# One product on VectorE takes the merge gates out of PSUM, in place of a ScalarE copy and a GpSimd product

## The chip, the cores and the metric

The kernel runs on one core of a Trainium2 chip. The metric is the device time of one execution in microseconds (us). The kernel before was run three times: 1630.13, 1631.73 and 1632.48 us, median 1631.73. The profile below is of one execution more.

TensorE is called PE here, VectorE DVE, ScalarE ACT, GpSimd POOL and SyncE SP, as the profile does. SP issues the DMA transfers.

## The reference

One decoder layer on x of 1024 tokens by 1024 channels, in float32: native sparse attention (NSA, three branches: compressed, selected, window) beside gated linear attention (GLA), both merged by per-channel gates, then a SwiGLU channel mixer. Cut to what matters for the change:

```
h = rmsnorm(x, gain)                       # rbc below: 1 / rms of each token
... = split(h @ w_in)                      # q, k, v, gates of both mixers, and g_merge (2 * 1024 columns)
o_a = nsa_attention(q, ...)                # 8 heads, 2 groups, query blocks of 128
o_b = gla(...)                             # chunk by chunk
gate_a, gate_b = split(sigmoid(g_merge))
merged = gate_a * (o_a @ w_up_nsa) + gate_b * (o_b @ w_up_gla)
x = x + merged @ w_out
```

The change concerns g_merge alone: its product with the weights stands in PSUM without the factor 1/rms of each token. It is multiplied by that factor and parked in DRAM until the merge takes the sigmoid of it.

## The kernel before, in words

Everything is laid out with channels on the 128 partitions and tokens along the row; a token row of 1024 is worked on in two halves of 512 (`hf`). Weights and activations are split in a high and a low part (`wh`, `wl`, `hh`, `hl`) so that float32 products are made of three matmuls. `dense` and `products` (L370 to L415) make a list of such work: a half of a job is 8 blocks of 3 matmuls of 128x512 (line L405) into one PSUM bank, then a call of `evac`, which takes the bank's content away and returns the word "pause". Each quarter of a job also loads weights (DMA), splits them by an ACT copy (L354) and a POOL subtraction (L355).

`gate_job(j)` is one job of this kind. For j below 4 it makes another gate, of the GLA mixer; for j of 4 to 19 it makes 128 channels of g_merge. Its `evac` copies PSUM to an SBUF tile `zt` on ACT (L926), multiplies it in place by `rbc`, 128x512, on POOL (L927), and stores it to DRAM on SP's queue (L928). There are 16 such jobs, 32 halves: two halves run in the GLA stage, two in the query stage (about 366 to 376 us), and 28 in the attention stage after it, up to about 738 us.

In the attention stage the merge gates are fill: PE works on them where attention isn't ready. The order of PE's work there is written by `Plan` (L107 to L236). It walks through 16 units of attention (2 groups of 8 query blocks) and keeps a simple model of when ACT, DVE and POOL will be done (`on`, `free`), with fixed costs in ns. At each step it takes a transpose (`turn`), scores (`score`) or a value product (`value`) that its model says is ready; where none is ready within 300 ns, it takes the next fill matmul. Fill has one PSUM bank, `d`; after the last matmul of a half ("pause") the plan gives no more fill until its model says that the bank is free (`self.d`). PE's order is fixed as `Plan` wrote it; the order on the other engines is made by a scheduler when the program is built, and each engine works through its own queue in order.

What attention puts on the engines, by lines of the profile: scores on PE into a bank of `s` (L1060 and L1061; L1040 for the compressed branch); maximum `nm` on DVE (L1101, L1088); exponential on ACT (L1103); reciprocal and weight `rr` on DVE (L1071, L1076); scaled `p` on DVE (L1079) or ACT (L1077); transposes on PE into one of two banks `t` (L1139, L1123); their split into `pth` by an ACT copy (L1116) and `ptl` by a DVE subtraction that reads the same bank (L1117); value products on PE (L1148, L1131). A bank `t` comes free when `ptl` is done. For each unit four casts on DVE (L1009) and POOL operations prepare the rotated queries `qs`.

Behind the attention stage the rest of the fill is worked off, then the merge reads the gates back from DRAM.

Of the kernel before, what the change touches and what calls it, by code (L numbers as in the profile page):

```python
# [14 lines left out]
AF = mybir.ActivationFunctionType  # L15
OP = mybir.AluOpType
AX = mybir.AxisListType.X

T, D, DFF = 1024, 1024, 2816
# [52 lines left out]
class Fill:  # L72
# [8 lines left out]
    def run(self, ns):  # L81
        self.credit += ns
        while self.q and self.credit > 0:
            cost, fn = self.q.popleft()
            self.credit -= cost
            fn()
        if not self.q:
            self.credit = 0.0
# [12 lines left out]
LAT, WAIT, LOADED = 155.0, 300.0, 1500.0  # L101
# [5 lines left out]
class Plan:  # L107
# [109 lines left out]
    def run(self):  # L217
        ops = dict(T=(self.turn_at, self.turn), S=(self.score_at, self.score), P=(self.value_at, self.value))
        while self.scores or self.turns or self.pend:
            at = {k: ops[k][0]() for k in ops}  # L220
            now = [k for k in ops if at[k] is not None and at[k] <= self.t]
            if now:
                ops[now[0]][1]()
                continue
            nxt = min((v, k) for k, v in at.items() if v is not None)
            if self.fill.q and self.d <= self.t and nxt[0] > self.t + WAIT:
                cost, fn = self.fill.q.popleft()
                self.t += cost
                said = fn()
                if said == "pause":  # L230
                    self.d = self.on("A", self.t, 478.0) + LAT
                elif said in ("part", "load"):
                    self.d = self.t + (LOADED if said == "load" else LOADED / 2)
                    self.on("A", self.t + 2500.0, 1040.0)
                continue
            self.t = nxt[0] if not self.fill.q or nxt[0] <= self.t + WAIT else min(nxt[0], self.d)  # L236
# [3 lines left out]
def layer_kernel(ctx, tc, a, outT):  # L240
    nc = tc.nc
    V, S, P, PE, SP = nc.vector, nc.scalar, nc.gpsimd, nc.tensor, nc.sync
# [54 lines left out]
    def mid(nm, dt=F32, shape=(512,)):  # L297
        return cur["pool"].tile([128, *shape], dt, name=nm, tag=cur["tag"], bufs=cur["bufs"])
# [10 lines left out]
    def hs(hf):  # L309
        return slice(512 * hf, 512 * (hf + 1))  # L310
# [148 lines left out]
    def log_sigmoid(out, z):  # L459
        S.activation(out, z, AF.Abs)  # L460
        S.activation(out, out, AF.Exp, scale=-1.0)
        S.activation(out, out, AF.Ln, bias=1.0)
        V.scalar_tensor_tensor(out, z, 0.0, out, op0=OP.min, op1=OP.subtract)
# [15 lines left out]
    rbc = cst.tile([128, 1024], F32, name="rbc")  # L479
# [83 lines left out]
    def proj(evac, bank=ps_m, fine=False):  # L563

        def make(getw):
            out = []
            for hf in range(2):
                out += products(getw, bank, hhf[hf], hlf[hf], 0,
                                lambda p, hf=hf: evac(p, hf), fine)
            return out  # L570
        return make
# [344 lines left out]
    def gate_job(j, bank=ps_m, fine=False):  # L916
        def evac(p, hf):
            t = mid("zt")
            if j < 4:
                e = mid("ze")  # L920
                V.tensor_mul(t, p, rbc[:, hs(hf)])
                log_sigmoid(e, t)
                S.activation(e, e, AF.Exp)
                P.tensor_tensor(t, t, e, OP.mult)
            else:
                S.activation(t, p, AF.Copy)  # L926
                P.tensor_tensor(t, t, rbc[:, hs(hf)], OP.mult)  # L927
            SP.dma_start(zd[j, :, hs(hf)], t)  # L928
        return a["w_t"][12 + j], proj(evac, bank, fine)

# [27 lines left out]
    for n, (h, hf) in enumerate(pieces):  # L958
# [14 lines left out]
        t = tz[:, 0, :]  # L973
# [772 lines left out]
```

## Time and profile before

| what | value |
|---|---|
| median of the runs | 1631.73 us (1630.13 to 1632.48) |
| the profiled execution: its own time | 1633.16 us |
| its span in the trace | 1631.4 us, so 1.76 us lie outside it |
| PE busy in the span | 1579.5 us, 97% |
| DVE, ACT, POOL busy in the span | 64%, 50%, 46% |
| attention stage (370 to 745 us): PE, DVE, ACT, POOL | 362.8, 274.2, 250.0, 154.2 us of 375 |

How to read it: an engine that is busy 97% leaves 3% in which it waited, and only there can a change of what the other engines do be seen in the time, as long as PE's own work stays the same. The view of waits says for each instruction how long its engine sat idle before it and whose end released it.

### The profile page before, as it was taken

Reading aid. Unit: us, or ns where it says so; the run is one execution under the profiler, and the core shown is the slowest. Engines: PE = TensorE matmul, PEld = TensorE weight load, DVE = VectorE, ACT = ScalarE, POOL = GpSimd, SP = SyncE. Lnnn points to the kernel's source line nnn. Section 1 sums busy time; section 2 is a strip of 40 time slices with the busy share of each in tenths; the row PEclk is TensorE's granted clock in tenths of the full one; section 3 lists DMA queues with packets and bytes.
Section 4 is the critical chain, followed back from the end, with each engine's and each line's share of the span. In section 5 each row is a group of like instructions: output and inputs, shape, how many; then the busy total and the mean of one; then the engine's idle time right before and its main releaser. Section 6 shows DMA issues by size and latency. Waiting matters only on the chain.

```text
span 1631.4 us, 23119 instructions
## 1 busy us (share of the span) xinstructions
PE 1579.5 (97%) x8047; PEld 1315.6 (81%) x8047; DVE 1050.3 (64%) x1704; ACT 815.4 (50%) x1643; POOL 747.0 (46%) x668
## 2 busy tenths in 40 slices
PE   9999999999999999998999999999999999999997
PEld 6888988887888878886777878888888888888886
DVE  7781587594876787778455477744444444499776
ACT  6132567454776666667644444333333334444542
POOL 6110376563333443434135440465666666646560
PEclk9999999999999999999999999999999999999999
DMA  5331122441111111121266541322332332695414
GB/s 196 112 100 57 61 67 70 132 149 62 44 45 46 53 49 40 36 89 64 92 200 231 188 155 56 128 101 98 103 100 101 103 104 97 218 369 162 142 43 145
DMA packets 107782, 179.85 MB, mean 110 GB/s; under 512 B 12033, under 2 KB 26770, under 8 KB 107666
## 3 DMA queue, kind: packets, MB, share of 16 engines
q1 hardware_dynamic: 104354, 172.35, 31.8%
q10 hardware_dynamic: 3312, 6.03, 1.0%
q8 instruction: 63, 1.03, 0.3%
q14 instruction: 53, 0.43, 0.1%
HBM read 130.36 MB, written 47.97 MB: 109 GB/s over the span
## 4 chain that ended last, share of the span: by engine, by line
PE 65%; DVE 7%; DMA 4%; ACT 4%; issue 3%; POOL 1%; SPq 1%; DVEq 0%; POOLq 0%; ACTq 0%
PE m L405 10%; PE m L1358 9%; PE m L1359 9%; PE m L1360 9%; PE d L405 7%; PE t L1139 3%; PE m L1675 3%; PE m L1677 3%; PE o L1148 3%; PE m L1676 3%; PE s L1060 2%; DVE qs L1009 1%; PE s L1061 1%; DMA ar<-actd 1%; DVE ptl L1117 1%
## 5 line engine op out<-in xcount | busy, mean ns | idle before, releaser
L355 POOL TENSOR_TENSOR wl<-wf,wh 128x512 fp32r<-128x512 f32 x106 | 146.1, 1382 | 295.4 <-ACT wh L354 267.8
L1358 PE MATMUL m<-xt,wh 128*128 128x512 f32 x412 | 161.4, 392 | 2.6 <-ACT sc L1364 2.6
L1360 PE MATMUL m<-xt,wl 128*128 128x512 f32 x412 | 160.3, 389 | 0.0
L1359 PE MATMUL m<-xt,wh 128*128 128x512 f32 x412 | 160.3, 389 | 0.0
L1291 POOL TENSOR_TENSOR wl<-ws,wh 128x512 fp32r<-128x512 f32 x76 | 107.4, 1418 | 91.2 <-ACT wh L1290 69.5
L1117 DVE TENSOR_TENSOR ptl<-t,pth 128x512 fp32r<-128x512 f32 (+1 forms) x168 | 99.6, 597 | 48.0 <-ACT pth L1116 44.8
L1291 POOL TENSOR_TENSOR wl<-wr,wh 128x512 fp32r<-128x512 f32 x69 | 91.6, 1328 | 58.5 <-ACT wh L1290 57.5
L1291 POOL TENSOR_TENSOR wl<-wd,wh 128x512 fp32r<-128x512 f32 x56 | 83.0, 1486 | 62.3 <-ACT wh L1290 62.1
L1290 ACT ACTIVATE wh<-wr 128x512 fp32r<-128x512 f32 x87 | 54.8, 630 | 111.8 <-POOL wl L1291 79.1
L1675 PE MATMUL m<-xb,wh 128*128 128x512 f32 x280 | 109.5, 391 | 0.3 <-DVE g L1405 0.3
L1291 DVE TENSOR_TENSOR xb<-ar,xb 128x512 fp32r<-128x512 f32 (+1 forms) x84 | 85.1, 1029 | 38.1 <-ACT xb L1290 37.9
L1677 PE MATMUL m<-xb,wl 128*128 128x512 f32 x280 | 109.3, 390 | 0.2 <-POOL wl L1291 0.2
L1676 PE MATMUL m<-xb,wh 128*128 128x512 f32 x280 | 109.0, 389 | 0.0
L354 ACT ACTIVATE wh<-wf 128x512 fp32r<-128x512 f32 x106 | 66.2, 627 | 82.0 <-PE m L405 48.3
L1116 ACT ACTIVATE pth<-t 128x512 fp32r<-128x512 f32 (+1 forms) x168 | 88.0, 526 | 37.1 <-PE t L1139 35.1
L1290 ACT ACTIVATE wh<-ws 128x512 fp32r<-128x512 f32 x76 | 47.9, 630 | 112.2 <-PE m L1359 93.1
L405 PE MATMUL m<-hh,wh 128*128 128x512 f32 x240 | 102.0, 425 | 0.0
L1139 PE MATMUL t<-ident,p 128*128 128x128 f32 x528 | 83.9, 276 | 13.1 <-DVE ptl L1117 13.0
L1358 PEld LDWEIGHTS m<-xt,wh 128*128 128x128 f32 x412 | 77.3, 188 | 22.1 <-ACT sc L1364 6.4
L405 PE MATMUL m<-hh,wl 128*128 128x512 f32 x240 | 94.1, 392 | 0.0
L405 PE MATMUL m<-hl,wh 128*128 128x512 f32 x240 | 93.9, 391 | 0.0
L1360 PEld LDWEIGHTS m<-xt,wl 128*128 128x128 f32 x412 | 77.3, 188 | 16.3
(385 smaller groups left out, 4657.1 us busy)
## 6 DMA issues: line engine op xcount, KB each, us to landing
ar<-actd SPq DMA_DIRECT2D x70, 256.0 KB, 3.1
wf<-in_w_t SPq DMA_DIRECT2D x58, 256.0 KB, 2.9
wr<-in_w_gate SPq DMA_DIRECT2D x44, 256.0 KB, 2.7
wr<-in_w_upf SPq DMA_DIRECT2D x44, 256.0 KB, 2.7
zd<-zt SPq DMA_DIRECT2D x40, 256.0 KB, 2.0
wd<-in_w_down SPq DMA_DIRECT2D x33, 256.0 KB, 5.2
wf<-in_w_out SPq DMA_DIRECT2D x32, 256.0 KB, 3.1
actd<-t SPq DMA_DIRECT2D x30, 256.0 KB, 2.0
```

Of the source, the lines that this page charges most:

```text
L355: (eng or V).tensor_tensor(wl, wf, f(wh), OP.subtract)
L405: PE.matmul(st["p"], w, x, start=k + i == 0, stop=k == n - 1 and i == 2)
L1117: V.tensor_tensor(tl[:, :c], pt[:, :c], f(th[:, :c]), OP.subtract)
L1139: PE.transpose(pt[:, bs(2 * b + par)], self.p[par][:, bs(kb + b)], ident)
L1290: S.activation(th, src, AF.Copy)
L1291: eng.tensor_tensor(tl, src, f(th), OP.subtract)
L1358: PE.matmul(ps, wh[:, c], xh, start=first and k == 0, stop=False, skip_group_check=not first)
L1359: PE.matmul(ps, wh[:, c], xl, start=False, stop=False, skip_group_check=not first)
L1360: PE.matmul(ps, wl[:, c], xh, start=False, stop=k == MH - 1, skip_group_check=not first)
L1675: PE.matmul(dst, wh[:, c], xh, start=first and p == 0, stop=False, skip_group_check=not first)
L1676: PE.matmul(dst, wh[:, c], xl, start=False, stop=False, skip_group_check=not first)
L1677: PE.matmul(dst, wl[:, c], xh, start=False, stop=p == NP - 1, skip_group_check=not first)
```

## The change

Two edits. In `gate_job`, the tile of a merge gate is now made by one DVE product that reads the bank `d` and `rbc` and writes `zt`. In `Plan`, the time at which the bank is taken to be free again after a half is worked out with 670 ns on DVE, where it was 478 ns on ACT. One line falls away, so that lines behind it have numbers lower by one in the changed kernel.

```diff
@@ Plan.run
                 said = fn()
                 if said == "pause":
-                    self.d = self.on("A", self.t, 478.0) + LAT
+                    self.d = self.on("D", self.t, 670.0) + LAT
@@ gate_job, evac
             else:
-                S.activation(t, p, AF.Copy)
-                P.tensor_tensor(t, t, rbc[:, hs(hf)], OP.mult)
+                V.tensor_mul(t, p, rbc[:, hs(hf)])
             SP.dma_start(zd[j, :, hs(hf)], t)
```

The queues change as follows at three places. DVE in the first unit of the attention stage, before (`ec` weights of the compressed branch, `qs` casts, `ptl` the split that frees a bank):

```order
L1048 TENSOR_TENSOR ec<-ec,rr_3385 128x256
L1009 CAST qs<-qa 64x256 x4
L1117 TENSOR_TENSOR ptl<-t,pth 128x256
L1101 TENSOR_REDUCE nm<-s 128x1 x2
L1071 RECIPROCAL rr<-z 128x1
```

and DVE at the same place of the changed kernel:

```order
L1047 TENSOR_TENSOR ec<-ec,rr_3381 128x256
L1008 CAST qs<-qa 64x256 x4
L926 TENSOR_TENSOR zt<-d,rbc 128x512
L1116 TENSOR_TENSOR ptl<-t,pth 128x256
L1100 TENSOR_REDUCE nm<-s 128x1 x2
```

The product stands between the casts and the first `ptl`. The second place is DVE near the end of the first group's units (about 551 us in the trace of before), before:

```order
L1163 TENSOR_TENSOR oa<-o,fo 64x2x128 x2
L1009 CAST qs<-qa 64x256 x4
L1088 TENSOR_REDUCE nm<-s 128x2
L1117 TENSOR_TENSOR ptl<-t,pth 128x256
L1071 RECIPROCAL rr<-z 128x2
L1076 TENSOR_TENSOR rr<-rr,gz 128x1
```

and in the changed kernel:

```order
L1162 TENSOR_TENSOR oa<-o,fo 64x2x128 x2
L926 TENSOR_TENSOR zt<-d,rbc 128x512
L1008 CAST qs<-qa 64x256 x3
L1116 TENSOR_TENSOR ptl<-t,pth 128x256
L1087 TENSOR_REDUCE nm<-s 128x2
L1008 CAST qs<-qa 64x256
L1116 TENSOR_TENSOR ptl<-t,pth 128x512
```

Here the product stands ahead of the casts, and the last cast and the maximum have moved behind the `ptl`. The third place is the first unit of the second group (about 593 to 598 us). PE there before, with the fill matmuls (L405) between two transposes:

```order
L1123 MATMUL t<-ident,ec 128x128 x2
L1148 MATMUL o<-pth,vs_1048 128x256
L1148 MATMUL o<-ptl,vs_1048 128x256
L405 MATMUL d<-hh,wl 128x512
...
L405 MATMUL d<-hh,wh 128x512
L1139 MATMUL t<-ident,p 128x128 x4
L1148 MATMUL o<-pth,vs_1048 128x256
```

Eleven fill matmuls stand between the value product and the four transposes. PE in the changed kernel:

```order
L1122 MATMUL t<-ident,ec 128x128 x2
L1147 MATMUL o<-pth,vs_1048 128x256
L1147 MATMUL o<-ptl,vs_1048 128x256
L405 MATMUL d<-hh,wh 128x512
L1138 MATMUL t<-ident,p 128x128 x4
L1147 MATMUL o<-pth,vs_1048 128x256
```

One is left there; two that stood ahead of the `ec` transposes are gone from there too, and the twelve follow later. DVE at this place before:

```order
L1076 TENSOR_TENSOR rr<-rr,gz 128x1
L1101 TENSOR_REDUCE nm<-s 128x1 x2
L1117 TENSOR_TENSOR ptl<-t,pth 128x256
L1071 RECIPROCAL rr<-z 128x1
L1117 TENSOR_TENSOR ptl<-t,pth 128x256
L1079 TENSOR_SCALAR p<-p,rr,gz 128x640
```

and in the changed kernel:

```order
L1075 TENSOR_TENSOR rr<-rr,gz 128x1
L1100 TENSOR_REDUCE nm<-s 128x1
L926 TENSOR_TENSOR zt<-d,rbc 128x512
L1070 RECIPROCAL rr<-z 128x1
L1100 TENSOR_REDUCE nm<-s 128x1
L1078 TENSOR_SCALAR p<-p,rr,gz 128x640
L1116 TENSOR_TENSOR ptl<-t,pth 128x256 x2
```

The two `ptl` have moved behind the product, the second maximum and the scaled `p`.

## Rows read from the trace of the kernel before

**Rows 1.** The page: engines' busy time; one group (busy, mean ns | idle before, releaser).

```profile
PE 1579.5 (97%) x8047; PEld 1315.6 (81%) x8047; DVE 1050.3 (64%) x1704; ACT 815.4 (50%) x1643; POOL 747.0 (46%) x668
...
L1117 DVE TENSOR_TENSOR ptl<-t,pth 128x512 fp32r<-128x512 f32 (+1 forms) x168 | 99.6, 597 | 48.0 <-ACT pth L1116 44.8
```

**Rows 2.** Waits of PE, 370 to 800 us: total us, times, longest.

```profile
PE t L1139 <- DVE ptl L1117: 13.0, 12, 2.1
...
PE o L1131 <- DVE ptl L1117: 1.8, 1, 1.8
```

**Rows 3.** Windows: us, busy of PE, PEld, DVE, ACT, POOL, PE's clock, DMA.

```profile
300.00:340.00 40.00, 40.00 (x212) 34.26 (x211) 26.04 (x39) 21.71 (x36) 22.00 (x22) 1.00 0.45 145
370.00:745.00 375.00, 362.82 (x2258) 306.84 (x2257) 274.24 (x614) 249.99 (x601) 154.24 (x160) 1.00 0.16 54
745.00:800.00 55.00, 46.82 (x286) 39.52 (x285) 39.53 (x100) 36.92 (x111) 10.78 (x12) 0.91 0.10 37
```

**Rows 4.** Groups by line and form, 370 to 745 us.

```profile
L927 POOL TENSOR_TENSOR zt<-zt,rbc 128x512 f32<-128x512 f32 x30 | 39.0, 1299 | 94.8 <-ACT zt L926 60.6 <-PE t L1139 16.6 <-issue 10.7
...
L926 ACT ACTIVATE zt<-d 128x512 f32<-128x512 f32 x28 | 16.4, 587 | 10.6 <-PE d L405 10.6
```

**Rows 5.** Lines L527 and L1009: durations in ns, least, median, most.

```profile
L527 DVE TENSOR_TENSOR krt<-m,rbc x4: 691/692/692, 73.6 to 119.0; 128x512 f32<-128x512 f32 x4
...
L1009 DVE CAST qs<-qa x64: 274/728/1368, 353.5 to 764.5; 64x256 fp32r<-64x256 f32 x64
```

**Rows 6.** Timeline 380 to 386 us: start, us, instruction, idle before and releaser.

```profile
385.23 0.42 DVE L1117 TENSOR_TENSOR ptl<-t,pth 128x256 fp32r<-128x256 f32 x1
...
385.71 0.50 PE L1131 MATMUL o<-ptl,vc 128*128 128x256 f32 x2 [1.83 <-DVE ptl L1117]
```

**Rows 7.** Timeline 453 to 457 us.

```profile
453.17 1.30 POOL L355 TENSOR_TENSOR wl<-wf,wh 128x512 fp32r<-128x512 f32 x1 [0.26 <-ACT wh L354]
453.32 0.67 DVE L1117 TENSOR_TENSOR ptl<-t,pth 128x512 fp32r<-128x512 f32 x1
...
454.40 1.54 DVE L1101 TENSOR_REDUCE nm<-s 128x1 f32<-128x640 f32 x2
...
455.42 0.58 ACT L926 ACTIVATE zt<-d 128x512 f32<-128x512 f32 x1
...
456.87 0.30 PE L1139 MATMUL t<-ident,p 128*128 128x128 f32 x1 [1.21 <-DVE ptl L1117]
```

**Rows 8.** Timeline 551 to 556 us.

```profile
553.15 1.33 POOL L927 TENSOR_TENSOR zt<-zt,rbc 128x512 f32<-128x512 f32 x1
...
555.84 0.41 PE L1139 MATMUL t<-ident,p 128*128 128x128 f32 x2 [1.44 <-DVE ptl L1117]
```

**Rows 9.** Chain of waits in 370 to 745 us: start, us, engine, output, line.

```profile
553.38 1.26 DVE qs L1009
...
742.08 1.27 DVE qs L1009
```

**Rows 10.** Timeline 581 to 584 us.

```profile
581.60 1.28 POOL L927 TENSOR_TENSOR zt<-zt,rbc 128x512 f32<-128x512 f32 x1
581.64 1.26 DVE L1076 TENSOR_TENSOR rr<-rr,gz 128x1 f32<-128x1 f32 x1
...
583.89 0.41 PE L1139 MATMUL t<-ident,p 128*128 128x128 f32 x2 [0.46 <-DVE ptl L1117]
```

**Rows 11.** Timeline 593 to 598 us.

```profile
593.85 1.65 DVE L1101 TENSOR_REDUCE nm<-s 128x1 f32<-128x640 f32 x2
...
595.46 0.40 PE L405 MATMUL d<-hh,wl 128*128 128x512 f32 x1
...
596.87 0.60 DVE L1079 TENSOR_SCALAR p<-p,rr,gz 128x640 f32<-128x640 f32 x1
...
597.58 0.16 DVE L1076 TENSOR_TENSOR rr<-rr,gz 128x1 f32<-128x1 f32 x1
...
597.98 0.60 PE L1139 MATMUL t<-ident,p 128*128 128x128 f32 x4
```

## The prediction

> **What bounds the kernel now.** I read the busy times first: PE is busy 97% of the span, DVE 64%, ACT 50%, POOL 46% [rows 1]. So the change, which touches only DVE, ACT and POOL, can move the time only through PE's idle 3% or by making more of it. Then the windows, to see which stage that is [rows 3]. In the GLA stage (300 to 340 us), where two of the halves fall, PE is busy 40.00 of 40.00 us. In the attention stage (370 to 745 us), where 28 fall, PE is busy 362.8 of 375 us, DVE 274.2 (73%), ACT 250.0, POOL 154.2: PE idles 12.2 us, DVE 100.8. Then PE's waits from 370 to 800 us [rows 2]: the transposes waited 13.0 us in 12 waits, and the value products 1.8 in one, for `ptl`, the DVE subtraction that frees a bank `t`. These 14.8 us are nearly all that there is to win. They hang on DVE's queue, and DVE itself most often waits for `pth` of ACT before a `ptl`: 44.8 of 48.0 us [rows 1].
>
> **The change part by part.** Durations are from the profiled execution, whose own time, 1633.16 us, is its span 1631.4 plus 1.76 outside it, and 1.43 over the median of the runs. I add to 1633.16 what PE's idle time changes by, and take 1.43 off.
>
> Removed in the attention stage: 28 ACT copies of 587 ns, 16.4 us, and the POOL products that belong to them, 28 of 1299 ns, 36.4 us (the row counts 30 and 39.0 because two halves of the query stage run into the window) [rows 4]. Both lie beside PE's work, so the 52.8 us are not a gain by themselves.
>
> Added: 28 DVE products. The same operation, one 128x512 input in PSUM and one in SBUF, stands in the trace already at L527 and takes 692 ns [rows 5]: 28 x 0.692 = 19.4 us. DVE goes from 274.2 to about 293 of 375 us, 78%. It stays below PE, and what decides is where in DVE's queue each product stands. If every one lay on PE's path the cost would be 19.4 (1651.1); if the change took away all 14.8 us of waits for `ptl` it would be 1616.9. Those are the two ends.
>
> The Trainium skill says under "VectorE: DVE Perf Modes", section "Specifications", that VectorE sits closer to SBUF and ScalarE closer to PSUM, which speaks against taking a tile out of PSUM on VectorE. The two rows agree, 692 against 587 ns [rows 4, 5]; by that rule alone the sum would be 28 x 0.105 = 2.9 us worse at most.
>
> Now the places, in order of time. The product goes in front of whatever stands behind it, and gives back what POOL and ACT did to DVE.
>
> (a) 385.7 us. PE waits 1.83 us for the first `ptl`, at 385.23 [rows 6]; the new order puts a product between the four casts and it: +0.69.
>
> (b) 455 us. PE waits 1.21 us for a `ptl` that came behind a `pth` that stood behind the ACT copy of 455.42 to 456.00 [rows 7]. The changed queue is product, one `nm`, `ptl`: the two `nm` begin at 454.40 and take 1.54 together, so from about 454.5 the product ends at 455.2, one `nm` at 456.0, the `ptl` of 0.42 [rows 6] at 456.4, where PE's start at 456.87 shows that it ended at about 456.7: -0.32. The pattern stands twice, the second time in the second group at 662 us: -0.32 again.
>
> (c) 551 to 556 us. PE waits 1.44 us for a `ptl` behind four casts [rows 8]. The last took 1.26 us at 553.38, while POOL was in the `zt` product of 553.15 to 554.48 [rows 8, 9]; the shortest of the casts takes 274 ns [rows 5]. With that product gone the cast is 0.98 shorter, and its successor, one cast, moves behind the `ptl`, while the DVE product lies beside a POOL operation that the casts waited out anyway: -1.0.
>
> (d) 583.9 us. A DVE operation on 128x1 took 1.26 us under the POOL product of 581.60 [rows 10], where its like takes 0.16 [rows 11]. The wait behind it, 0.46, goes: -0.46.
>
> (e) 725 to 745 us. Here the chain of waits runs through DVE, and three products fall into it: 3 x 0.69 = +2.07. One cast of 1.27 us there [rows 9] is again one beside a POOL `zt` product: back to 0.28, -0.99. Together +1.1.
>
> (f) 593 to 598 us. The plan's new cost moves fill: before the four transposes of 597.98 there stand twelve matmuls fewer. They took 0.229 us each (eleven from 595.46 to 597.98 [rows 11]), so PE comes 2.75 us earlier to transposes that need a bank `t`. In the queue of before the `ptl` that frees it is done at 595.9, right behind the two `nm` of 593.85 to 595.50; now it stands behind `nm`, product, `nm` and the `p` of 0.60. From 593.85: 0.82 + 0.69 + 0.16 + 0.82 + 0.60 + 0.42 = 597.4, with the waits for the exponential between them 597.7. So the transposes can't start before about 597.75, 0.23 earlier than they did: a new wait of 2.75 - 0.23 = +2.5. The matmuls that were there come later and change nothing by themselves.
>
> That makes nine of the 28 products (one each in a, c, d and f, two in b, three in e). For the other 19 I take nothing: they fall into DVE's 100.8 us of idle time, or behind the `ptl` that PE waits for. If that cover were gone, each costs 0.69. The two halves of the GLA stage are hidden by PE's full queue, and PE doesn't wait for the two of the query stage; without cover 4 x 0.69 = 2.8.
>
> The product itself could be held up by POOL, as the casts are. The `ptl` at 453.32, which also reads one input from PSUM, took 0.67 us right under a POOL operation of 1.30 us [rows 7], so I take 0.69 everywhere; held up as the cast was, a product would cost up to 1.0 more at the places above. The Trainium skill, "SBUF — State Buffer", section "Who interferes with whom", says that a VectorE instruction with at most one SBUF input outside the two-port modes doesn't contend with GpSimd, while casts do and then block fully. Both rows agree with it. By that rule the nine products stay at 0.69, and every cast caught under a `zt` product gains what (c) and (e) count, so the sum by it is the one here.
>
> Sum: 0.69 - 0.64 - 1.0 - 0.46 + 1.1 + 2.5 = +2.2 us. 1633.16 + 2.2 - 1.43 = 1633.9 us, 0.13% above the median.
>
> **The rivals.**
>
> *DVE's queue becomes what PE waits for (slower).* One mechanism: a `ptl` that PE waits for stands behind a product, and PE waits longer by its 0.69. There are 13 such waits. For it: DVE is at 73% with 28 more operations to come, and the order on DVE is fixed when the program is built, so that a product whose bank isn't full yet holds up what is behind it. Against it: DVE stands idle 44.8 us before its `ptl` waiting for ACT [rows 1], and a product can hide in that. If it happens at seven of the 13, 4.8 us, and the hole of (f) opens, 2.5, while (b) to (d) give nothing back, the time is 1631.7 + 7.3 = 1639.0. It decides from the second such wait on, since 2.5 + 2 x 0.69 = 3.9 is the first sum to pass 3.3 us, 0.2%. In the tail behind 745 us, where the clock is granted at 0.91 [rows 3], longer pauses of PE could add a stretch at the lower level; that is why the range ends above this.
>
> *Relief of ACT and POOL decides (faster).* ACT loses 16.4 us and POOL 36.4, and 44.8 us of DVE's idle time before `ptl` ends with an ACT copy [rows 1, 4]. If the `pth` come earlier by the 0.59 of the copy wherever one stood before them, and the slowed DVE operations of (c), (d) and (e) go back, half of the 13.0 us of waits would go: 1631.7 - 6.5 = 1625.2. For it: three of the operations that were slowed lie in the chain itself. Against it: only in (b) did I find an ACT copy of `zt` right ahead of a `pth` that PE waited for, and the product comes in the copy's stead on the engine that `ptl` needs too.
>
> *No hole in (f) (no change).* If the bank `t` is free in time after all, because the scaled `p` gets its exponential sooner with the ACT copy gone, the other terms leave -0.3: 1631.4.
>
> **How the numbers follow.** My forecast 0.36, the first rival 0.28, relief 0.20, no hole 0.15, the rest 0.01. What a measurement of this kernel can tell from no change is about 0.2%, 3.3 us: 1628.5 to 1635.0. The forecast's own range is 2 us to either side, so 0.26 of its 0.36 falls within and 0.10 above. No hole counts as within, 0.15. The first rival is above with 0.26 and within with 0.02; relief is below with 0.19 and within with 0.01. So: faster 0.19 (+0.01 for the rest) = 0.20, same 0.44, slower 0.36. The range takes in the relief's 1625.2 in good part and the first rival with a lower stretch of the clock of a microsecond or two: 1626 to 1641.
>
> **What would show it.** In the profile after: DVE busy about 293 us in the attention stage, products of 0.69 us, POOL and ACT down by 36 and 16. In PE's waits, a new one of about 2.5 us for `ptl` at the first unit of the second group, a wait of about 2.5 in place of 1.83 in the first unit, none at the place of 583.9. In the line of the casts the longest ones fewer. It would be wrong if PE waited for the product itself (the bank `d`), if the waits for `ptl` fell below 9 us in all (relief), or if they were over 18 (the first rival).

## The result, and the profile after

The changed kernel takes 1622.82 us (median of seven runs, 1620.56 to 1625.34), the kernel before 1630.48 us beside it (seven runs, 1627.50 to 1635.47). The ratio is 0.9950, 95% interval 0.9932 to 0.9967: faster by 0.5%, about 8 us. I had forecast 1633.9 us, no measurable change, and a range from 1626 on. The direction, the time and the range were wrong.

The profiled execution took 1621.17 us, its span is 1619.4 us: 12.0 us less than the span of before. The engines' busy times, to be read beside [rows 1]:

```profile
PE 1575.2 (97%) x8047; PEld 1312.5 (81%) x8047; DVE 1054.8 (65%) x1736; ACT 798.8 (49%) x1611; POOL 702.3 (43%) x636
```

PE executes the same 8047 matmuls, but is busy for 4.3 us less. That can't come from waits; it is the first sign that in these two executions the clock has a part in it. The windows (us, busy time of PE, its weight loads, DVE, ACT, POOL, granted clock, DMA), beside [rows 3]:

```profile
370.00:745.00 375.00, 365.08 (x2285) 308.39 (x2283) 290.41 (x655) 239.90 (x583) 117.87 (x132) 1.00 0.16 53
745.00:800.00 55.00, 50.49 (x307) 42.64 (x307) 35.32 (x94) 37.42 (x110) 10.89 (x11) 1.00 0.18 66
```

DVE has risen to 290.4 us and POOL has fallen by 36.4, both as counted; ACT fell by 10.1, less than the 16.4 removed: it has 18 instructions fewer in the window and not 28, so other work moved in. PE is idle 9.9 us between 370 and 745 us, 12.2 before. Behind 745 us the clock is granted at 1.00, where it was 0.91. PE's waits from 370 to 800 us, beside [rows 2]:

```profile
PE t L1138 <- DVE ptl L1116: 8.6, 8, 2.0
PE o L1130 <- DVE oa L1162: 2.1, 3, 0.8
PE o L1130 <- DVE ptl L1116: 2.0, 1, 2.0
```

The waits for `ptl` in these rows are 10.6 us in nine places, where they were 14.8 in 13; one of 0.5 us, of the `ec` transposes, has come. And the new operation itself, by line (count, busy us, mean ns, then DVE's idle time ahead of it and its releaser), with the size that [rows 5] gave:

```profile
L926 DVE TENSOR_TENSOR zt<-d,rbc 128x512 f32<-128x512 f32 x28 | 19.2, 685 | 14.5 <-PE d L405 14.2
```

**The ledger.** Between 360 and 800 us PE's busy time is 419.6 of 440 us before and 425.6 after; idle 20.4 and 14.4. The clock's part is the sum, over windows of 1 us there, of one less the granted clock: 5.1 us before and 0 after. So the 12.0 us by which the two spans differ are 6.0 of waits and 5.1 of clock in this window, and about 1 that isn't attributed. Over the whole span PE's idle time fell by 7.7 us (51.9 to 44.2), the same sum for the clock only from 12.5 to 10.1 us, since outside this window the changed kernel has more of it, 10.1 us against 7.4 (near 56, 295, 868 and 943 us and at its end). The rows that carry the clock's part in the window stand in the tail of the kernel before: the waits there (start, us, instruction, idle before it and its releaser),

```profile
769.39 0.80 PE L1139 MATMUL t<-ident,p 128*128 128x128 f32 x4 [2.08 <-DVE ptl L1117]
784.26 0.77 PE L1131 MATMUL o<-pth,vc 128*128 128x256 f32 x2 [2.44 <-DVE oa L1163]
```

and the windows behind them, in which the granted clock falls to its lower level, 1.2 GHz (0.50; the first window begins at the higher one):

```profile
768.00:772.00 4.00, 2.61 (x14) 2.55 (x15) 2.92 (x9) 3.28 (x9) 0.00 (x0) 0.71 0.18 66
784.00:788.00 4.00, 3.74 (x19) 3.77 (x19) 2.31 (x8) 1.86 (x7) 0.00 (x0) 0.50 0.19 72
```

In the changed kernel the same transposes don't wait (759.60 us in its trace) and the same value product waits 0.80 us,

```profile
772.25 0.47 PE L1130 MATMUL o<-pth,vc 128*128 128x256 f32 x2 [0.80 <-DVE oa L1162]
```

and between 360 and 800 us its clock is granted at 1.00 throughout.

**All runs.** Two profiled executions can differ by luck of the clock (5.1 and 3.4 us in two of the kernel before, see e8), but every run on record has its span and its mean granted clock. One less that clock, times the span, is the clock's part of the run; the clock is given to three decimals, so only means over runs are of use. The changed kernel's seven runs have 10.7 us of it in the mean (clocks of 0.992 to 0.995), the 82 runs of the kernel before that were made beside the experiments 11.3 us (0.988 to 0.997). Without it the spans are 1610.5 and 1618.1 us. So of the 8 us about 7.6 are not the clock's, as much as PE's idle time fell by, and 0.6 us, no more than the scatter of these means, are.

### The profile page after: what moved, and what is told of

Read it like the earlier page. It is cut to its first block, busy times and chain, and to the rows that moved or that the text cites. A ratio compares the mean times of both kernels' runs of the same rounds, so it can differ in the third digit from the quotient of the medians.

```text
span 1619.4 us, 23066 instructions
## 1 busy us (share of the span) xinstructions
PE 1575.2 (97%) x8047; PEld 1312.5 (81%) x8047; DVE 1054.8 (65%) x1736; ACT 798.8 (49%) x1611; POOL 702.3 (43%) x636
## 4 chain that ended last, share of the span: by engine, by line
PE 72%; DVE 6%; ACT 2%; issue 2%; DMA 2%; POOL 1%; SPq 0%; DVEq 0%; POOLq 0%; ACTq 0%
PE m L405 10%; PE m L1357 9%; PE d L405 9%; PE m L1358 9%; PE m L1359 9%; PE m L1674 4%; PE m L1675 4%; PE m L1676 4%; PE o L1147 3%; PE t L1138 3%; PE s L1059 2%; PE s L1060 2%; DVE ptl L1116 1%; DMA u<-ud 1%; PE t L836 1%
## 5 line engine op out<-in xcount | busy, mean ns | idle before, releaser
L355 POOL TENSOR_TENSOR wl<-wf,wh 128x512 fp32r<-128x512 f32 x106 | 144.2, 1363 | 367.3 <-ACT wh L354 350.1
L405 PE MATMUL m<-hh,wh 128*128 128x512 f32 x240 | 102.6, 427 | 0.0
L405 PE MATMUL m<-hh,wl 128*128 128x512 f32 x240 | 94.8, 395 | 0.0
L405 PE MATMUL m<-hl,wh 128*128 128x512 f32 x240 | 94.6, 394 | 0.0
```

The lines of the kernel that those rows point to most:

```text
L355: (eng or V).tensor_tensor(wl, wf, f(wh), OP.subtract)
L405: PE.matmul(st["p"], w, x, start=k + i == 0, stop=k == n - 1 and i == 2)
```

## The experiments

Two theories stood at first. **R** (relief): ACT's copy and POOL's product are out of the way of what PE waits for. **F** (fill): the plan's new cost puts fill matmuls where PE would wait, and the product is neutral. PE's order depends on `Plan` alone, so the change splits cleanly: e1 has PE's order of the changed kernel, e2 that of before.

"Idle" is 440 us less PE's busy time in the window of 360 to 800 us; "clock" the sum defined above for that window; both are of the one profiled execution. "Rest" is over all runs: the mean span without the clock's part, less the same of the runs of before made beside it (for the changed kernel, of all 82). It is an estimate, with a standard error of 0.4 to 0.8 us.

| kernel | ratio to before | 95% interval | idle, us | clock, us | rest, us |
|---|---|---|---|---|---|
| before | 1 | | 20.4 | 5.1 | 0 |
| e8 before, again | (one run) | | 20.1 | 3.4 | (one run) |
| changed kernel | 0.9950 | 0.9932 to 0.9967 | 14.4 | 0 | -7.6 |
| e1 plan alone | 0.9971 | 0.9959 to 0.9984 | 16.2 | 6.8 | -3.2 |
| e2 product alone | 0.9981 | 0.9970 to 0.9992 | 19.5 | 5.1 | -2.9 |
| e3 changed, POOL's product back | 0.9976 | 0.9962 to 0.9989 | 17.7 | 0 | -3.3 |
| e4 changed, ACT's copy back | 0.9967 | 0.9955 to 0.9979 | 15.9 | 1.7 | -4.7 |
| e5 changed, up projection on the old cost | 0.9939 | 0.9925 to 0.9953 | 14.8 | 1.7 | -7.3 |
| e6 before, `oal` on POOL | 0.9977 | 0.9965 to 0.9989 | 20.3 | 1.7 | 0.0 |
| e7 changed, `oal` on POOL | 0.9946 | 0.9926 to 0.9966 | 15.0 | 0 | -6.6 |
| e9 product, plan 478 on DVE | 0.9919 | 0.9902 to 0.9935 | 13.2 | 0 | -7.6 |
| e10 product, plan 670 on ACT | 0.9984 | 0.9970 to 0.9998 | 18.6 | 6.8 | -4.3 |
| e11 product, plan 850 on DVE | 0.9950 | 0.9935 to 0.9965 | 14.0 | 1.7 | -7.5 |
| e12 product, plan counts nothing | 1.0516 | 1.0495 to 1.0537 | 54.6 | 11.9 | +57.4 |
| e13 product, DVE charged in place of ACT, old bank time | 0.9953 | 0.9941 to 0.9966 | 13.9 | 3.4 | -7.3 |
| e14 product, new bank time, ACT charged as before, DVE not | 0.9968 | 0.9955 to 0.9980 | 16.4 | 5.1 | -6.4 |
| e15 old copy and product, plan 478 on DVE | 0.9971 | 0.9957 to 0.9984 | 17.3 | 1.7 | -2.4 |

**e1, the plan's edit alone.** The kernel before with

```diff
-                    self.d = self.on("A", self.t, 478.0) + LAT
+                    self.d = self.on("D", self.t, 670.0) + LAT
```

> The plan's new cost (670 ns on DVE) with the old ScalarE copy and GpSimd product: PE's order is that of the changed kernel. Theory R (relief: what counts is that ScalarE's copy and GpSimd's product are out of the way of what PE waits for): no gain, a hole of about 1.5 us before the four transposes of the second group's first unit, so 1630 to 1633 us, ratio 1.000 to 1.002. Theory F (fill: fourteen fill matmuls later and other gaps filled; the product itself is neutral): most of the 7.7 us are here already, about 1624 us, ratio 0.996.

Measured: 1626.72 us against 1630.78, ratio 0.9971. Neither theory's number: this edit alone gives 4.7 us (0.0029 of 1630.78), somewhat more than half. A new wait does open at the second group's first unit,

```profile
601.18 0.63 PE L1139 MATMUL t<-ident,p 128*128 128x128 f32 x4 [1.11 <-DVE ptl L1117]
```

but PE's waits fall in all (to be read beside [rows 2]):

```profile
PE t L1139 <- DVE ptl L1117: 9.5, 10, 2.2
PE o L1131 <- DVE ptl L1117: 1.8, 1, 1.8
PE o L1131 <- DVE oa L1163: 1.5, 2, 0.8
```

One place where they went is 455 us, (b) of the prediction. In before a run of 13 fill matmuls stands ahead of four transposes at 445.0 us and nine behind them ahead of the next ones; with the new plan 15 and seven. All that follows on DVE and POOL is spaced otherwise: in before the split of weights (POOL, L355) lay on DVE's `rr`, which took 0.57 us:

```profile
453.17 1.30 POOL L355 TENSOR_TENSOR wl<-wf,wh 128x512 fp32r<-128x512 f32 x1 [0.26 <-ACT wh L354]
453.91 0.57 DVE L1076 TENSOR_TENSOR rr<-rr,gz 128x1 f32<-128x1 f32 x1
```

With the plan's edit, the old copy and product still in place, `rr` takes 0.16 us, the split coming 0.7 us after its start, and the transposes behind it, which waited 1.21 us [rows 7], stand with no wait shown:

```profile
456.23 0.16 DVE L1076 TENSOR_TENSOR rr<-rr,gz 128x1 f32<-128x1 f32 x1
...
458.99 0.63 PE L1139 MATMUL t<-ident,p 128*128 128x128 f32 x4
```

**e2, the product alone.** The changed kernel with the plan's line as in before.

> The product on VectorE with the old plan: PE's order is that of the kernel before, row for row. Theory R: the whole gain and a little more, since the new hole of 2.0 us in the second group's first unit can't open: about 1621 us, ratio 0.994. Theory F: 1629 to 1632 us, ratio 0.999 to 1.001. My prediction's own terms without (f) would give -0.3 us.

Measured: 1627.42 us, ratio 0.9981. Faster too, by 3.1 us (1.3 to 4.9): less than theory R had put on it, more than theory F. Together e1 and e2 make 0.9952; the change is at 0.9950: the two edits add up, within their intervals. Idle time falls by only 0.8 us here (1.5 over the whole span), less than the time; the rest column has 2.9, so the clock isn't the cause of that, and it stays open. The two long waits of the old tail are still there, untouched by the product:

```profile
769.15 0.63 PE L1138 MATMUL t<-ident,p 128*128 128x128 f32 x4 [2.08 <-DVE ptl L1116]
782.46 0.76 PE L1130 MATMUL o<-pth,vc 128*128 128x256 f32 x2 [2.44 <-DVE oa L1162]
```

So it is PE's new order that takes them away, not the relief of ACT or POOL.

**e3 and e4, one half of the relief taken back.** The changed kernel, with one operation on the tile itself behind the product (in e3 the factor is applied twice; in e4 the copy changes nothing):

```diff
                 V.tensor_mul(t, p, rbc[:, hs(hf)])
+                P.tensor_tensor(t, t, rbc[:, hs(hf)], OP.mult)     # e3
+                S.activation(t, t, AF.Copy)                        # e4
```

> The changed kernel with GpSimd's product put back behind VectorE's (the factor is applied twice); PE's order as in the changed kernel. If GpSimd's relief (slowed VectorE casts and small operations) is what gives the time: 3 to 5 us slower than the changed kernel, about 1627 us, ratio 0.998. If ScalarE's relief or the order of the queues gives it: no change from the changed kernel, ratio 0.995.

> The changed kernel with a ScalarE copy of the tile onto itself put back behind VectorE's product; PE's order as in the changed kernel. If ScalarE's relief gives the time (pth no longer behind a copy of 0.59 us): 3 to 5 us slower than the changed kernel, about 1627 us, ratio 0.998. If GpSimd's relief or the fill gives it: no change, ratio 0.995.

Measured: 1627.17 us (0.9976) and 1626.88 us (0.9967), idle 17.7 and 15.9 against 14.4. Putting POOL's product back costs 3.3 us of waits in the profiled execution, ACT's copy 1.5. The intervals of the two times overlap with each other and, at their edges, with the changed kernel's; the rest column is clearer, 4.3 us for POOL's product and 2.9 for ACT's copy. So both reliefs are real, and POOL's seems the larger. They don't add up: e1, with both operations back and no product on DVE, is 4.4 us above the changed kernel in that column. Place (c) shows POOL's: in e3 the wait of PE is

```profile
554.63 0.44 PE L1139 MATMUL t<-ident,p 128*128 128x128 f32 x2 [2.13 <-DVE ptl L1117]
```

and in the changed kernel, PE's order being the same,

```profile
552.82 0.44 PE L1138 MATMUL t<-ident,p 128*128 128x128 f32 x2 [1.22 <-DVE ptl L1116]
```

**e5, which pauses of the plan count.** The changed kernel, but the plan counts the old 478 ns on ACT behind the halves of the up projection, whose tile ACT still copies.

> The changed kernel, but after a half of the other fill job of the tail (the up projection, whose tile ScalarE still copies) the plan counts the old 478 ns on ScalarE; PE's order is that of the changed kernel up to about 730 us and differs by 22 rows behind. If the tail's gain comes from the plan's new cost at the merge gates (fill put elsewhere ahead of the tail): about 1623 to 1625 us, ratio 0.995 to 0.996, no waits over 2 us behind 745 us. If it comes from the new cost behind the up projection's halves: the two long waits of the old tail (2.1 and 2.4 us) come back, about 1627 to 1629 us, ratio 0.998.

Measured: 1622.40 us, 0.9939. In its time as the first alternative had it: the gain is that of the merge gates' pauses. Of the two long waits of the old tail the one for `oa` came back (2.3 us), so that one does hang on the up projection's pauses; the one for `ptl` didn't.

**e6 and e7, VectorE's queue in the tail.** `oal`, the low part of the attention output `oa`, is made by a subtraction on DVE. Here that of the first group is put on POOL, in the kernel before (e6) and in the changed one (e7):

```diff
-                V.tensor_tensor(tl[:, hs(hf)], oa[g][hf][:, j, :], f(th[:, hs(hf)]), OP.subtract)
+                (V if g else P).tensor_tensor(tl[:, hs(hf)], oa[g][hf][:, j, :], f(th[:, hs(hf)]), OP.subtract)
```

> The kernel before, with the four subtractions oal of the first group (L1218) on GpSimd in place of VectorE; PE's order is that of before. Theory Q (the long waits of the old tail are made by what VectorE's queue has ahead of the ptl, here two oal of 2.33 us together): the waits at 766.9 and perhaps 781.6 go or shrink below 1.5 us, PE's clock doesn't fall behind them, and the time is 4 to 6 us below before, about 1626 us, ratio 0.997. Theory F (PE's order alone: too little fill at those places): the waits stay, ratio 1.000.

> The changed kernel with the same four subtractions on GpSimd. Theory Q: the wait of 1.58 us at about 755 us, which stands behind two oal of 1.97 us, goes: 1 to 2 us faster than the changed kernel, about 1621 us, ratio 0.994. Theory F: no change from the changed kernel, 0.995.

Measured: e6 1628.55 us, 0.9977; e7 1623.60 us, 0.9946, no change from the changed kernel (its wait at that place grew from 1.58 to 2.71 us instead of going). In e6 the waits of the old tail became shorter, though not under 1.5 us:

```profile
767.75 0.63 PE L1139 MATMUL t<-ident,p 128*128 128x128 f32 x4 [1.55 <-DVE ptl L1117]
778.33 0.63 PE L1139 MATMUL t<-ident,p 128*128 128x128 f32 x4 [0.94 <-DVE ptl L1117]
781.20 0.48 PE L1131 MATMUL o<-pth,vc 128*128 128x256 f32 x2 [1.70 <-DVE oa L1163]
```

PE's idle time in all is that of before, 20.3 us, and still the kernel is 3.8 us faster (1.8 to 5.7). What fell in the profiled execution is the clock's part, 1.7 us against 5.1 and 3.4. All runs agree: without the clock's part e6 is as long as before (0.0, with a standard error of 0.7 us), and its mean granted clock is 0.9941 where that of the 13 runs of before beside it is 0.9920, which is 3.5 us less of the clock's part (standard error 1.2). That fits that a long pause costs more than itself; that it is these two pauses which did it rests on the fit.

**e8, the kernel before once more.**

> The kernel before once more, for its trace. If the stretches at the lower clock behind the waits at 766.9 and 781.6 us belong to the order of work, they stand there again. If a pause of this length only sometimes lets the clock fall, they stand elsewhere or are fewer, and PE's waits are the same to 0.2 us.

Measured: PE's waits are the same, the two in the tail to 0.01 us:

```profile
767.97 0.63 PE L1139 MATMUL t<-ident,p 128*128 128x128 f32 x4 [2.08 <-DVE ptl L1117]
782.84 0.77 PE L1131 MATMUL o<-pth,vc 128*128 128x256 f32 x2 [2.44 <-DVE oa L1163]
```

The clock fell behind both again, but for 3.4 us of loss against 5.1:

```profile
768.00:772.00 4.00, 4.00 (x21) 3.62 (x22) 2.53 (x7) 2.61 (x9) 0.00 (x0) 0.64 0.19 70
784.00:788.00 4.00, 4.00 (x25) 3.74 (x23) 1.49 (x5) 1.81 (x6) 0.00 (x0) 0.72 0.02 6
```

**e9 to e12, is it the number, the engine or luck.** VectorE's product with four forms of the plan's line:

```diff
-                    self.d = self.on("D", self.t, 670.0) + LAT
+                    self.d = self.on("D", self.t, 478.0) + LAT     # e9
+                    self.d = self.on("A", self.t, 670.0) + LAT     # e10
+                    self.d = self.on("D", self.t, 850.0) + LAT     # e11
+                    self.d = self.t + LAT                          # e12
```

> VectorE's product; after a half the plan counts the old 478 ns, but on VectorE. Theory E (what helps is that the plan waits for the busier of the two engines before it gives the bank fill again): the gain of the changed kernel stays, about 1623 us, ratio 0.995, PE's idle time from 360 to 800 us near the changed kernel's 14.5 us. Theory C (it is the longer cost): as with the old plan, about 1627 us, 0.998, idle time near 19.5 us. Theory L (one order happens to fit and the others don't): anything between, without a pattern.

> VectorE's product; the plan counts 670 ns, but on ScalarE. PE's order differs from that of before by 12 rows only. Theory E: as with the old plan, about 1627 us, ratio 0.998, idle time near 19.5 us. Theory C: the gain stays, 0.995.

> VectorE's product; the plan counts 850 ns on VectorE. PE's order differs from that of the changed kernel by 44 rows. Theory E: like the changed kernel, 0.994 to 0.996. Theory C: the same or a little better. Theory L: anywhere from 0.994 to 1.000.

> VectorE's product; after a half the plan counts nothing but its 155 ns, so that fill follows at once where a gap is, and PE waits for the bank itself. Theory E: waits of PE for the bank d appear and the waits for ptl are not fewer, slower than with the old plan: over 1628 us, ratio above 0.998. Theory L: anywhere. If the bank is in truth free at once, as fast as the changed kernel, 0.995.

Measured: 1617.30, 1627.54, 1622.89 and 1714.46 us. Theory E holds: 478, 670 and 850 ns on DVE give 0.9919, 0.9950 and 0.9950, 478 and 670 ns on ACT 0.9981 and 0.9984. In the rest column these are -7.6, -7.6 and -7.5 against -2.9 and -4.3. The length counts little, the engine much. With no count at all PE stands in front of the bank, since the product that empties it waits in DVE's queue (first rows of PE's waits in e12):

```profile
PE d L405 <- DVE zt L926: 39.4, 27, 4.1
PE d L405 <- ACT zt L1178: 12.9, 9, 2.8
```

e9 is the fastest kernel here, 13 us below before and below the changed kernel, with intervals that touch only at their ends (0.9902 to 0.9935, 0.9932 to 0.9967). Its waits for `ptl` are 8.7 us, 10.6 in the changed kernel:

```profile
PE t L1138 <- DVE ptl L1116: 6.7, 8, 1.6
PE o L1130 <- DVE ptl L1116: 2.0, 1, 2.0
```

But without the clock's part it is no faster than the changed kernel. Its four runs have mean clocks of 0.996 to 0.998, 4.4 us of the clock's part against 10.7 (and 9.2 in e11, made beside it): what e9 is ahead by is the clock, and four runs don't tell whether that would last.

**e13 to e15, which effect of the plan's edit.** Still open was whether it is the later bank or the charge on the model of DVE. VectorE's product in e13 and e14, the old copy and product in e15:

```diff
-                    self.d = self.on("D", self.t, 670.0) + LAT
+                    self.d = max(self.free["A"], self.t + LAT) + 478.0 + LAT    # e13
+                    self.on("D", self.t, 670.0)                                 # e13
+                    self.d = max(self.free["D"], self.t + LAT) + 670.0 + LAT    # e14
+                    self.on("A", self.t, 478.0)                                 # e14
+                    self.d = self.on("D", self.t, 478.0) + LAT                  # e15
```

> VectorE's product; in the plan the bank comes free as by the old rule (478 ns behind what ScalarE has to do), but VectorE's account is charged with 670 ns. Theory V (charging VectorE is what helps): near the changed kernel, 1620 to 1624 us, ratio 0.993 to 0.996, PE's idle time from 360 to 800 us 13 to 15 us. Theory B (the later bank is what helps): as with the old plan, 1627 us, 0.998, idle 18 to 20 us.

> VectorE's product; the bank comes free by the new rule (670 ns behind what VectorE has to do), but ScalarE's account is charged with the old 478 ns and VectorE's with nothing. Theory V: as with the old plan, 1627 us, ratio 0.998, idle 18 to 20 us. Theory B: near the changed kernel, 0.993 to 0.996, idle 13 to 15 us.

> The old ScalarE copy and GpSimd product with the plan that counts 478 ns on VectorE; PE's order is that of the fastest kernel so far (e9). If the two edits add up as in e1 and e2, the product's share of about 3 to 4 us is missing: about 1621 us, ratio 0.994 to 0.996. If the order alone does it: 0.992.

Measured: 1623.27 (0.9953), 1624.94 (0.9968) and 1626.67 us (0.9971). Charging DVE gives the changed kernel's time and its idle time (13.9 us), as theory V had it; but e13's line also leaves ACT without its old charge, and no run parts the two. The later bank alone lies between, 16.4 us idle and -6.4 us in the rest column, so it has most of the gain and isn't without effect, as theory V had put it. e15 lacks the product, and with it more than I had expected: 8.5 us against e9 (0.0052 of 1631), with an idle time of 17.3 against 13.2; 5.2 us of it are left in the rest column, and the remainder is e9's clock.

## Why the prediction was wrong

**What held.** The bound: PE's waits in 360 to 800 us are where most of the change acted (6.0 of 7.7 us of idle time), 3.7 us of it in those for `ptl`. The product's size, 692 ns expected, 685 measured. (f): twelve matmuls fewer ahead of the four transposes, and a new wait of 2.5 us; it is there, 2.04 us, behind product, `nm`, `p` and two `ptl` as laid out:

```profile
590.60 0.68 DVE L926 TENSOR_TENSOR zt<-d,rbc 128x512 f32<-128x512 f32 x1
...
592.80 0.60 DVE L1078 TENSOR_SCALAR p<-p,rr,gz 128x640 f32<-128x640 f32 x1
...
593.32 0.75 DVE L1116 TENSOR_TENSOR ptl<-t,pth 128x256 fp32r<-128x256 f32 x2
...
593.89 0.63 PE L1138 MATMUL t<-ident,p 128*128 128x128 f32 x4 [2.04 <-DVE ptl L1116]
```

e1 has 1.11 us of it without any product, so the plan makes the larger part. None of the signs by which the prediction was to be known as wrong appeared: the waits for `ptl` are 11.1 us in all, between its bounds of 9 and 18. They looked at waits for `ptl` in all and for the bank `d`, and the time moved elsewhere too.

**The product's terms, by e2**, whose PE order is that of before. (a) was 0.69: the wait went from 1.83 to 2.11 us, +0.28. (b) was -0.32 twice: the waits of 1.21 us are 1.05 and 0.75. (c) was -1.0: -0.54; under the new plan it is as large as forecast, 2.24 us in e1, 2.13 in e3 and 1.22 in the changed kernel. (d) was -0.46: gone. (e) was +1.1: PE's idle time from 720 to 745 us went from 2.5 to 4.1, +1.6, but behind 745 us, where no term stood, it fell by 1.3. In sum -0.3 forecast without (f), -0.8 of idle time measured. The signs are right; the time moved by -3.1 us, more than the waits, with an interval that reaches up to -1.3. So the product's gain was sized too small as well (-0.3 for -3.1 us), and where the 2 us arise that PE's waits don't show stays open.

**The step that failed** is the last sentence of (f): "The matmuls that were there come later and change nothing by themselves." I followed the fill at one place, where it left a hole, and costed the rest of PE's new order at nothing. In place of the +2.5 us of (f), e1 shows that the new order is worth -4.7 us, hole included (-3.2 without the clock's part). The two waits of (b), 1.21 us each, and two of 0.66 went, one of 0.84 came; of the long waits of the tail the one of 2.08 us went and the one of 2.44 is 0.80, while new ones came there of at most 1.59. Not every wait fell: that of (c) grew from 1.44 to 2.24 us. The clock I had only as a loss: I let it widen the range upward, and read a granted clock of 0.91 behind 745 us [rows 3] without asking what pauses stood ahead of it and whether they would stay. In the profiled executions that was 5.1 of the 12.0 us; over all runs it was about 0.6 of the 8, so it is not why the forecast failed.

**The rival** that came true in direction is relief, put at 1625.2 us with a chance of 0.20. Its mechanism is only a part: e3 and e4 give it 3.3 and 1.5 us of waits, POOL's share seeming the larger, where I had argued mainly from ACT's `pth`; relief alone, with the old order of PE, came to 1627.4 us (e2). For the sentence on the Trainium skill, "SBUF — State Buffer", section "Who interferes with whom": the trace agrees, since the 28 products with one input in PSUM took 672 to 692 ns, the seven that lay beside POOL's work no longer than the others, and in the changed kernel the median of the 64 casts fell from 728 ns [rows 5] to

```profile
L1008 DVE CAST qs<-qa x64: 273/466/1379, 353.3 to 754.3; 64x256 fp32r<-64x256 f32 x64
```

The 0.10 us by which the product on VectorE is longer than the copy on ScalarE was not seen in PE's waits: in the changed kernel none of them is put down to the product.

**Not settled.** Which part of the plan's edit helps: the charge on DVE, ACT without its charge, or the later bank. Why the product alone gives more time than PE's waits show. Whether e9's clock would last: its order lacks the wait of (f), but it is one order among many, and I wouldn't expect the number to carry over.

## What to carry to other kernels

Where a planner writes the order of the bottleneck engine, an edit to its costs is a change of its own: run it alone before reading the other half of the diff. Charge an operation to the engine that executes it (e10 against the changed kernel and e11: 0.9984 against 0.9950, with the same product); the reason may be that the plan then expects what is queued behind it later and fills the gap ahead of it, which is argued and not shown. And look at the granted clock behind the longest pauses, since shortening these can give back more than the pause (e6); but before a gain is put down to the clock, compare the mean clock of all runs, since one profiled execution of each kernel can differ by luck.

## What the runs showed of the hardware

The same pause at the same place may or may not be followed by a lower clock. Behind the first `ptl` at 385 us e1 waited 1.84 us and its clock fell to 0.50 (wait, then the window behind it):

```profile
385.97 0.50 PE L1131 MATMUL o<-ptl,vc 128*128 128x256 f32 x2 [1.84 <-DVE ptl L1117]
```

```profile
388.00:392.00 4.00, 3.66 (x11) 2.87 (x12) 2.25 (x7) 2.38 (x7) 0.25 (x1) 0.50 0.17 66
```

The changed kernel waited 2.04 us there, and its clock stayed at 1.00, with twice the matmuls in the window:

```profile
385.54 0.50 PE L1130 MATMUL o<-ptl,vc 128*128 128x256 f32 x2 [2.04 <-DVE ptl L1116]
```

```profile
388.00:392.00 4.00, 4.00 (x22) 3.14 (x22) 2.69 (x7) 3.13 (x6) 0.00 (x0) 1.00 0.00 0
```

Such stretches cost 1.7 or 3.4 us each by the sum defined above. They make a large part of the 8 us or so by which runs of one kernel differ: the two fastest of e7's six runs, 1619.95 and 1620.31 us, had a mean granted clock of 0.996, the two slowest, 1627.22 and 1629.71, of 0.991 and 0.990.
